# The last token tile's right half of the down projection as two pieces of 256 columns

## The chip, the core and the metric

The kernel is one program on one core of one Trainium2 chip. The metric is the device time of one execution in microseconds (us), taken as the median of several executions. The profile is of one more execution; its span runs from the first instruction to the last.

## The reference

The reference is one layer of a hybrid decoder on 512 tokens of 1024 channels: a norm, three parallel token mixers, gates, an output projection, and then a gated MLP with a short convolution. The change touches only the last two lines, the MLP's down projection with its residual and the final norm over each token's 1024 channels:

```python
def rms_norm(x, gain):
    x32 = x.astype(jnp.float32)
    y = x32 * lax.rsqrt(jnp.mean(x32 * x32, axis=-1, keepdims=True) + EPS)
    return (y * gain.astype(jnp.float32)).astype(x.dtype)
...
    x = x + (jax.nn.gelu(gate_h, approximate=True) * val_h) @ w_down[l]
return rms_norm(x, final_norm)
```

## The kernel before

The 512 tokens are four tiles of 128, t = 0 to 3; a tile is 128 partitions. The 1024 channels are two halves of 512 columns, c = 0 (left) and c = 1 (right). `x2[t][c]` holds the residual stream. Most of the down projection is added to `x2` earlier, by `down_fast`. What is left are the last 512 of its 3072 inner rows, `group(20)`, and this is the very end of the program: `down_units(wdown2, group(20), final, None, final_left, 2)`.

Each fp32 product is made of three matmuls by `mm3` (L104): both operands are split into a high and a low part, in the page's names `whi`/`wlo` or `r`. For a token tile and a half there are 2 weight tiles (`nk` = 2) of 2 blocks, so 4 terms and 12 matmuls of 128x512, all into one bank of PSUM, the accumulator memory.

The left halves are made first by `token_units`, for all four tiles in four banks. The right halves follow in `token_held`, tile by tile, each in a bank of its own. After each tile's 12 matmuls `evac` runs: DVE adds the bank into `x2[t][1]` (L1107), ACT squares it and sums along the row into `msq[t][:, 1:2]` (`meansq`, L124; the row READ_ACCUMULATOR belongs to it), and `final(t)` makes the row's scale `y`: a square root on ACT (L1378) and four small steps on DVE (L1379 to L1382, with `y` from L1382). The left half's part of the mean square came before, in `final_left(t)`, which also multiplied the left half by the gain on POOL (`xl`). Then the left half is scaled by `y` on ACT (L1389) and stored (L1390), and the right half is scaled on DVE by `y` and the gain (L1386, inner function `right`) and stored (L1387).

The order on DVE is set by hand around these steps. For t < 3, `final` puts its last DVE step (L1382) in `queue` and `right` in `late`. The next tile's `evac` takes them out: its add is issued after that step of the tile before, and the tile before's `right` is issued after the add. So DVE does, in this order: scale of tile t (L1379 to L1382), add of tile t + 1, `right` of tile t. For t = 3 `right` runs at once, and the left store goes out from ACT's queue; all other stores go out from SyncE's (SP's). Engines take their instructions in order, and a wait holds everything behind it on that engine.

Of the kernel before, what the change touches and what calls it, by code (L numbers as in the profile page):

```python
# [13 lines left out]
AF = mybir.ActivationFunctionType  # L14
ALU = mybir.AluOpType
# [3 lines left out]
P = 128  # L19
D = 1024  # L20
KD = D // P
S = 512
NT = S // P
# [34 lines left out]
def trunk(ctx: ExitStack, tc: tile.TileContext, x, xT, mem, memT, par, wdecay, wch, wv, wg, wmk,  # L58
          wmv, wrg, wbr, wout, wup, wdown, wdown2, gffn, gfin, out):
    nc = tc.nc  # L60
# [11 lines left out]
    def nm(s):  # L72
        uid[0] += 1
        return f"{s}_{uid[0]}"

    def fslot(shape=(P, S)):
        return apool.tile(list(shape), F32, tag="s", name=nm("f"))
# [7 lines left out]
    def bank(shape=(P, S)):  # L85
        return psm.tile(list(shape), F32, tag="mm", name=nm("mm"))

    def sbank(shape=(P, S)):
        return pss.tile(list(shape), F32, tag="sm", name=nm("sm"))

    def stat(n, p=P):
        return small.tile([p, n], F32, tag=f"st{n}", name=nm("st"), bufs=12)
# [7 lines left out]
    def mm3(ps, terms, first=True, last=True, more=False):  # L100

        seq = [p for a, b, c, d in terms for p in ((a, c), (a, d))] + [(b, c) for a, b, c, d in terms]
        for i, (l, r) in enumerate(seq):
            nc.tensor.matmul(ps, lhsT=l, rhs=r, start=first and i == 0,  # L104
                             stop=last and i == len(seq) - 1, skip_group_check=more)
# [15 lines left out]
    def meansq(src, acc, width):  # L121

        junk = small.tile([P, src.shape[-1]], BF16, tag="junk", name=nm("junk"), bufs=2)
        nc.scalar.activation(junk, src, AF.Square, scale=width ** -0.5, accum_out=acc)  # L124
# [8 lines left out]
    def unit(dram, n, fn, parts=1):  # L133

        w = {}
        i = sum(1 for k, *_ in prog if k == "unit")

        def ready():
            w["w"] = fetch(dram, n, parts)
            for h in behind.get(i, ()):  # L140
                h()
        prog.append(("unit", [(AHEAD, ready)], lambda: fn(w["w"])))
# [5 lines left out]
    def step(fn):  # L148
        prog.append(("step", [], fn))

    def weave(units, steps, lead=0):

        done, m = 0, max(1, len(units) - lead)
        for i, u in enumerate(units):
            unit(*u)
            upto = len(steps) * max(0, i + 1 - lead) // m
            for s in steps[done:upto]:
                step(s)
            done = max(done, upto)
        for s in steps[done:]:  # L160
            step(s)
# [36 lines left out]
    HB = D // 2  # L198
# [10 lines left out]
    ps = sbank((P, P))  # L209
# [38 lines left out]
    def token_units(dram, n, lhs, nt, evac, nk=4):  # L248

        pst = []  # L250

        def fn(i, w):
            if i == 0:
                pst.extend(bank((P, n)) for _ in range(nt))
            for t in range(nt):
                mm3(pst[t], [(*lhs(2 * i + j, t), *w(j, 2)) for j in range(2)], i == 0, i == nk - 1)
                if i == nk - 1:
                    evac(t, pst[t])
        return [(dram[i], 2 * n, lambda w, i=i: fn(i, w)) for i in range(nk)]

    def token_held(dram, n, lhs, nt, evac, between=None, nk=4):

        ws = []

        def fn(i, w):
            ws.append(w)
            if i < nk - 1:
                return
            for t in range(nt):
                ps = bank((P, n))  # L270
                for c in range(nk):
                    mm3(ps, [(*lhs(2 * c + j, t), *ws[c](j, 2)) for j in range(2)], c == 0, c == nk - 1)
                    if c == 0 and t >= 2 and between is not None:
                        between(t - 2)
                evac(t, ps)
        return [(dram[i], 2 * n, lambda w, i=i: fn(i, w), 2) for i in range(nk)]
# [274 lines left out]
    xr = [None] * NB  # L551
# [533 lines left out]
    x2 = [[None, None] for _ in range(NT)]  # L1085
# [6 lines left out]
    gb = {}  # L1092

    def gain_rows(src):
        for j in range(2):
            gb[j] = fslot()
            with tc.issue_after(loads[-1].ins):
                nc.sync.dma_start(gb[j], src[:, j * HB:(j + 1) * HB])

    msq, queue, late = {}, [], []  # L1100

    def down_units(wd, acts, after, between=None, left=None, nk=4):

        def evac(t, ps, c):

            with tc.issue_after(queue.pop()) if queue else ExitStack():
                add = nc.vector.tensor_tensor(out=x2[t][c], in0=x2[t][c], in1=ps, op=ALU.add)  # L1107
            while late:
                with tc.issue_after(add.ins):
                    late.pop()()  # L1110
            if c == 0:
                msq[t] = stat(2)
            meansq(x2[t][c], msq[t][:, c:c + 1], D)
            if c == 1:
                after(t)
            elif left is not None:
                left(t)
        lhs = lambda k, t: tuple(a[:, t * P:(t + 1) * P] for a in acts(k))
        add = lambda c: lambda t, ps: evac(t, ps, c)
        return token_units(wd[0], HB, lhs, NT, add(0), nk) + token_held(wd[1], HB, lhs, NT, add(1), between, nk)  # L1120

    def rstd(t):
        tot, ss = stat(1), msq.pop(t)
# [32 lines left out]

    step(lambda: gain_rows(gffn))
    wo = down_units(wout, lambda k: mr[k], norm2, norm2_flip)
    step(lambda: residual(0))
    weave(wo[:4], [])  # L1160
# [209 lines left out]

    lefts = {}

    def final(t):
        b, xl = lefts.pop(t)
        ss = msq.pop(t)

        root, h, y, u = stat(1), stat(1), stat(1), stat(1)
        nc.scalar.activation(root, ss[:, 1:2], AF.Sqrt, bias=b)  # L1378
        nc.vector.tensor_scalar(out=h, in0=ss[:, 1:2], scalar1=b, scalar2=-0.5, op0=ALU.add, op1=ALU.mult)  # L1379
        nc.vector.reciprocal(y, root)  # L1380
        nc.vector.scalar_tensor_tensor(out=u, in0=y, scalar=h, in1=y, op0=ALU.mult, op1=ALU.mult)
        last = nc.vector.scalar_tensor_tensor(out=y, in0=u, scalar=1.5, in1=y, op0=ALU.add, op1=ALU.mult)  # L1382

        def right():
            xr = fslot()
            nc.vector.scalar_tensor_tensor(out=xr, in0=x2[t][1], scalar=y, in1=gb[1], op0=ALU.mult, op1=ALU.mult)  # L1386
            nc.sync.dma_start(out[t * P:(t + 1) * P, HB:], xr)  # L1387

        nc.scalar.activation(xl, xl, AF.Copy, scale=y)  # L1389
        (nc.sync if t < NT - 1 else nc.scalar).dma_start(out[t * P:(t + 1) * P, :HB], xl)  # L1390
        if t < NT - 1:
            queue.append(last.ins)
            late.append(right)
        else:
            right()

    acts = {}

# [7 lines left out]
    group = lambda first: lambda k: acts[first + k]  # L1406
# [14 lines left out]
    blend(us[2:], down_fast(0, 3, group(0), True, False))  # L1421
    blend(up_units(range(20, NF), halves), down_fast(3, 2, group(12), False, True))
    step(lambda: gain_rows(gfin))
    weave(down_units(wdown2, group(20), final, None, final_left, 2), [])

    emit()

# [90 lines left out]
```

## Time and profile before

| | us |
|---|---|
| median of 3 runs | 923.41 |
| lowest and highest of them | 923.1, 926.32 |
| profiled execution, its own time | 924.37 |
| span of the profiled execution | 922.6 |
| end of the last matmul, from the start of the span | 915.66 |

The profiled execution's time is 1.8 us more than its span, and 0.96 us over the median. Rows give a start in us from the start of the span, then a length. Matmuls are pipelined: the next starts before the one before has ended, so the step from start to start is shorter than the length of one.

### The profile page before, as it was taken

To read this page: it belongs to the slowest core of one execution; us is meant where nothing else is said; L and a number is where in the kernel's file an instruction comes from. 1 tells how busy PE (TensorE), PEld (TensorE's weight loads), DVE (VectorE), ACT (ScalarE), POOL (GpSimd) and SP (SyncE) were. 2 spreads that over 40 slices of the span, in tenths; PEclk is the share of its full clock that TensorE was granted. 3 is DMA by queue.
4 is the path that set the end of the run, shared out by engine and by line. 5 is a ranking of instruction groups with operands and counts; after the bars stand their busy time and mean duration, and the time that the engine had idled before them with its cause. 6 is when DMAs were issued, how large, how long until landed. Compare 5 with 4: busy or idle time off the path is not lost.

```text
span 922.6 us, 12732 instructions
## 1 busy us (share of the span) xinstructions
PE 912.0 (99%) x4606; PEld 784.1 (85%) x4606; DVE 657.2 (71%) x1168; ACT 524.1 (57%) x888; POOL 128.1 (14%) x168
## 2 busy tenths in 40 slices
PE   9999999999999999999999999999999999999997
PEld 7899888888889998888888898998988888888885
DVE  6997755665689568746766678767787757598765
ACT  7765655685865468474534446555555445445544
POOL 0010000000243430320000000222111130013102
PEclk9999999999999999999999999999999999999998
DMA  7446223213467884321157313675646785357622
GB/s 238 148 137 214 92 88 101 88 42 119 110 170 167 187 204 126 115 86 53 52 157 258 116 59 90 157 185 130 148 114 165 145 228 125 114 137 181 139 69 91
DMA packets 51183, 123.27 MB, mean 134 GB/s; under 512 B 6145, under 2 KB 14001, under 8 KB 51121
## 3 DMA queue, kind: packets, MB, share of 16 engines
q1 hardware_dynamic: 35648, 94.99, 31.6%
q0 software_dynamic: 15328, 27.21, 17.3%
q8 instruction: 36, 0.59, 0.3%
q10 hardware_dynamic: 144, 0.26, 0.1%
q14 instruction: 27, 0.21, 0.1%
HBM read 117.99 MB, written 3.67 MB: 132 GB/s over the span
## 4 chain that ended last, share of the span: by engine, by line
PE 87%; DMA 5%; DVE 3%; issue 2%; ACT 2%; POOL 0%; SPq 0%; DVEq 0%; POOLq 0%; ACTq 0%
PE mm L104 78%; DMA f<-in_wup 4%; PE sm L104 3%; DMA f<-in_wv 2%; PE mm L436 2%; DVE wlo L98 1%; DVE r L98 1%; ACT r L97 1%; PE sm L211 0%; PE sm L996 0%; PE sm L983 0%; PE sm L1010 0%; DVE f L810 0%; PE sm L1147 0%; PE sm L601 0%
## 5 line engine op out<-in xcount | busy, mean ns | idle before, releaser
L97 ACT ACTIVATE whi<-raw 128x1024 fp32r<-128x1024 f32 (+3 forms) x142 | 135.5, 961 | 144.4 <-PE mm L104 113.1
L98 DVE TENSOR_TENSOR wlo<-raw,whi 128x1024 fp32r<-128x1024 f32 (+3 forms) x142 | 157.4, 1113 | 82.8 <-ACT whi L97 39.4
L104 PE MATMUL mm<-whi,r 128*128 128x512 f32 (+2 forms) x568 | 171.2, 372 | 0.0
L104 PEld LDWEIGHTS mm<-whi,r 128*128 128x128 f32 x568 | 105.5, 188 | 15.9 <-ACT r L97 0.3
L104 PE MATMUL mm<-hh,whi 128*128 128x512 f32 x288 | 113.4, 394 | 0.0
L104 PE MATMUL mm<-hl,whi 128*128 128x512 f32 x288 | 112.8, 392 | 0.0
L104 PE MATMUL mm<-wlo,r 128*128 128x512 f32 (+2 forms) x284 | 105.7, 372 | 0.5 <-DVE wlo L98 0.5
L104 PE MATMUL mm<-h2l,whi 128*128 128x512 f32 x264 | 102.8, 390 | 0.0
L104 PE MATMUL mm<-h2h,whi 128*128 128x512 f32 x264 | 102.7, 390 | 0.0
L98 DVE TENSOR_TENSOR r<-f,r 128x512 fp32r<-128x512 f32 (+3 forms) x144 | 79.7, 577 | 23.0 <-ACT r L97 22.7
L104 PE MATMUL mm<-r,whi 128*128 128x512 f32 (+1 forms) x432 | 94.2, 367 | 0.0
L97 ACT ACTIVATE r<-f 128x512 fp32r<-128x512 f32 (+3 forms) x144 | 70.1, 535 | 34.1 <-DMA f<-in_wup 29.2
L98 DVE TENSOR_TENSOR wlo<-f,whi 128x512 fp32r<-128x512 f32 (+2 forms) x90 | 53.8, 631 | 47.5 <-ACT whi L97 40.6
L104 PEld LDWEIGHTS mm<-r,whi 128*128 128x128 f32 x432 | 75.2, 189 | 13.1
L97 ACT ACTIVATE whi<-f 128x512 fp32r<-128x512 f32 (+2 forms) x90 | 48.2, 579 | 62.5 <-PE mm L104 48.8
L104 PE MATMUL mm<-hh,wlo 128*128 128x512 f32 x288 | 71.4, 390 | 0.0
L104 PE MATMUL mm<-r,r 128*128 128x512 f32 (+2 forms) x336 | 65.7, 346 | 0.3 <-ACT r L97 0.3
L104 PE MATMUL mm<-h2h,wlo 128*128 128x512 f32 x264 | 65.2, 389 | 0.0
L104 PEld LDWEIGHTS mm<-hh,wlo 128*128 128x128 f32 x288 | 54.0, 188 | 11.2
L104 PEld LDWEIGHTS mm<-hh,whi 128*128 128x128 f32 x288 | 54.1, 188 | 10.8
L104 PEld LDWEIGHTS mm<-hl,whi 128*128 128x128 f32 x288 | 54.1, 188 | 10.7
L104 PEld LDWEIGHTS mm<-r,r 128*128 128x128 f32 (+1 forms) x336 | 53.3, 186 | 9.6 <-ACT r L97 0.5
(261 smaller groups left out, 1545.2 us busy)
## 6 DMA issues: line engine op xcount, KB each, us to landing
raw<-in_wch SPq DMA_DIRECT2D x39, 512.0 KB, 3.3
raw<-in_wup SPq DMA_DIRECT2D x36, 512.0 KB, 4.0
f<-in_wdown POOLq DMA_DIRECT2D x40, 256.0 KB, 7.0
raw<-in_wbr SPq DMA_DIRECT2D x24, 384.0 KB, 3.1
raw<-in_wdown SPq DMA_DIRECT2D x14, 512.0 KB, 3.8
f<-in_wup SPq DMA_DIRECT2D x24, 256.0 KB, 6.9
f<-in_wup POOLq DMA_DIRECT2D x24, 256.0 KB, 6.4
f<-in_wdown SPq DMA_DIRECT2D x20, 256.0 KB, 4.7
```

What stands on the lines that cost most here:

```text
L97: nc.scalar.activation(hi, src, AF.Copy)
L98: return (eng or nc.vector).tensor_tensor(out=lo, in0=src, in1=hi.bitcast(F32), op=ALU.subtract)
L104: nc.tensor.matmul(ps, lhsT=l, rhs=r, start=first and i == 0, stop=last and i == len(seq) - 1, skip_group_check=more)
L436: nc.tensor.matmul(ps[u], lhsT=w(a, u, k), rhs=xs["r"][k][j], start=k == 0 and i < n, stop=k == KD - 1 and i >= len(seq) - n)
```

## The change

Tile 3's right half is made in two pieces of 256 columns, h = 0 and 1, in the two halves of the same bank: 12 matmuls of 128x256 for the first piece, then 12 for the second. After each piece `last` adds the 256 columns into `x2[3][1]` and squares them. The first piece's square sum goes to `msq[3]` as before; `final_quarter` adds it to the left half's on DVE and gives the second piece a sum of its own. The second piece then calls `final(3)`, which makes `y` as before, and scales both halves in pieces of 256 columns, each with a store of its own (128 KB in place of 256 KB): one store from ACT's queue, three from SP's. `queue` and `late` are emptied at the first piece's add.

```diff
+                if last is not None and t == nt - 1:
+                    for h in range(2):
+                        cols = slice(h * n // 2, (h + 1) * n // 2)
+                        mm3(ps[:, cols], [(*lhs(2 * c + j, t), *(a[:, cols] for a in ws[c](j, 2)))
+                                          for c in range(nk) for j in range(2)])
+                        last(cols, ps[:, cols])
+                    return
...
+        def last(cols, ps):
+            t, x = NT - 1, x2[NT - 1][1][:, cols]
+            with tc.issue_after(queue.pop()) if queue else ExitStack():
+                add = nc.vector.tensor_tensor(out=x, in0=x, in1=ps, op=ALU.add)
+            while late:
+                with tc.issue_after(add.ins):
+                    late.pop()()
+            meansq(x, msq[t][:, 1:2], D)
+            (quarter if cols.start == 0 else after)(t)
...
+    def final_quarter(t):
+        b, xl = lefts[t]
+        lefts[t] = stat(1), xl
+        nc.vector.tensor_tensor(out=lefts[t][0], in0=b, in1=msq[t][:, 1:2], op=ALU.add)
+        msq[t] = stat(2)
...
+        xr = fslot()
+        for h in range(2):
+            c = slice(h * HB // 2, (h + 1) * HB // 2)
+            nc.scalar.activation(xl[:, c], xl[:, c], AF.Copy, scale=y)
+            nc.vector.scalar_tensor_tensor(out=xr[:, c], in0=x2[t][1][:, c], scalar=y, in1=gb[1][:, c],
+                                           op0=ALU.mult, op1=ALU.mult)
+            (nc.scalar if h else nc.sync).dma_start(out[rows, c], xl[:, c])
+            nc.sync.dma_start(out[rows, HB + c.start:HB + c.stop], xr[:, c])
...
-    weave(down_units(wdown2, group(20), final, None, final_left, 2), [])
+    weave(down_units(wdown2, group(20), final, None, final_left, 2, final_quarter), [])
```

On every engine the order up to tile 3's right half is the same. The line numbers of the changed kernel are higher: its add of a piece is L1130, the sum of the squares L1395, the scale L1404 to L1407, `right` of tile 2 L1413 and of tile 3 L1427. In brackets stands the engine whose count an instruction waits for.

On PE, before, tile 3's right half (bank `mm_8649`) begins so:

```order
L104 MATMUL mm_8649<-r_8458,r_7878 128x512 [waits DVE_49]
L104 MATMUL mm_8649<-r_8459,r_7878 128x512
L104 MATMUL mm_8649<-r_8462,r_8072 128x512
L104 MATMUL mm_8649<-r_8463,r_8072 128x512
L104 MATMUL mm_8649<-r_8458,r_7879 128x512
```

On PE, in the changed kernel, the last three matmuls of the first piece and the first three of the second:

```order
L104 MATMUL mm_8649<-r_8462,r_8073 128x256
L104 MATMUL mm_8649<-r_8496,r_8229 128x256
L104 MATMUL mm_8649<-r_8500,r_8411 128x256
L104 MATMUL mm_8649<-r_8458,r_7878 128x256 [waits DVE_49]
L104 MATMUL mm_8649<-r_8459,r_7878 128x256
L104 MATMUL mm_8649<-r_8462,r_8072 128x256
```

There are now 24 matmuls of half the columns, and the second piece's first one waits for DVE; in the built program the count that it waits for is that of the first piece's add.

On DVE, before, from the last step of tile 2's scale to the end of the program (`m_4828` is tile 3's right half, `f_8663` tile 2's result):

```order
L1382 SCALAR_TENSOR_TENSOR st_8640<-st_8641,st_8640 128x1 [waits DVE_49]
L1107 TENSOR_TENSOR m_4828<-m_4828,mm_8649 128x512 [waits PE_49]
L1386 SCALAR_TENSOR_TENSOR f_8663<-m_4826,st_8640,f_8454 128x512 [waits DVE_49]
L1379 TENSOR_SCALAR st_8669<-st_8555,st_8558 128x1 [waits Activation_49]
L1380 RECIPROCAL st_8670<-st_8668 128x1 [waits Activation_49]
L1381 SCALAR_TENSOR_TENSOR st_8671<-st_8670,st_8669 128x1 [waits DVE_49]
L1382 SCALAR_TENSOR_TENSOR st_8670<-st_8671,st_8670 128x1 [waits DVE_49]
L1386 SCALAR_TENSOR_TENSOR f_8679<-m_4828,st_8670,f_8454 128x512 [waits DVE_49]
```

On DVE, in the changed kernel, the same stretch:

```order
L1407 SCALAR_TENSOR_TENSOR st_8640<-st_8641,st_8640 128x1 [waits DVE_49]
L1130 TENSOR_TENSOR m_4828<-m_4828,mm_8649 128x256 [waits PE_49]
L1413 SCALAR_TENSOR_TENSOR f_8663<-m_4826,st_8640,f_8454 128x512 [waits DVE_49]
L1395 TENSOR_TENSOR st_8668<-st_8558,st_8555 128x1 [waits Activation_49]
L1130 TENSOR_TENSOR m_4828<-m_4828,mm_8649 128x256 [waits PE_49]
L1404 TENSOR_SCALAR st_8687<-st_8670,st_8668 128x1 [waits Activation_49]
L1405 RECIPROCAL st_8688<-st_8686 128x1 [waits Activation_49]
L1406 SCALAR_TENSOR_TENSOR st_8689<-st_8688,st_8687 128x1 [waits DVE_49]
L1407 SCALAR_TENSOR_TENSOR st_8688<-st_8689,st_8688 128x1 [waits DVE_49]
L1427 SCALAR_TENSOR_TENSOR f_8695<-m_4828,st_8688,f_8454 128x256 [waits DVE_49]
L1427 SCALAR_TENSOR_TENSOR f_8695<-m_4828,st_8688,f_8454 128x256
```

The first piece's add stands where the whole add stood, behind tile 2's scale; the second piece's add stands behind tile 2's `right` and behind L1395, which waits for ACT's square of the first piece.

On SP, in the changed kernel, the last six stores (`f_8633`, `f_8546` and `f_8663` are of tiles 1 and 2, `f_8695` is tile 3's right half, `f_8560` its left):

```order
L1414 DMA out<-f_8633 128x512 [waits DMAHW4_49,DVE_49]
L1418 DMA out<-f_8546 128x512 [waits DMAHW5_49,Activation_49]
L1414 DMA out<-f_8663 128x512 [waits DMAHW6_49,DVE_49]
L1430 DMA out<-f_8695 128x256 [waits DMAHW7_49,DVE_49]
L1429 DMA out<-f_8560 128x256 [waits DMAHW1_49,Activation_49]
L1430 DMA out<-f_8695 128x256 [waits DMAHW2_49,DVE_49]
```

Where one store of tile 3 stood there are three; the fourth, of the left half's second piece, is ACT's.

## Rows read from the trace of the kernel before

**Rows 1.** The page: busy share of PE, and the engines' shares of the chain.

```profile
PE 912.0 (99%) x4606; PEld 784.1 (85%) x4606; DVE 657.2 (71%) x1168; ACT 524.1 (57%) x888; POOL 128.1 (14%) x168
...
PE 87%; DMA 5%; DVE 3%; issue 2%; ACT 2%; POOL 0%; SPq 0%; DVEq 0%; POOLq 0%; ACTq 0%
```

**Rows 2.** The chain that ended last, from 912.8 us: start, length, what.

```profile
912.72 2.96 PE mm L104 x13
...
915.70 0.70 DVE m L1107
...
916.42 0.73 ACT junk L124 x2
...
918.21 0.72 ACT f L1389
```

**Rows 3.** Timeline of PE, the four right halves: start, length, operation, count.

```profile
904.62 11.04 PE L104 MATMUL mm<-r,r 128*128 128x512 f32 x48
```

**Rows 4.** Timeline of the end, ACT, DVE and the stores' issues.

```profile
915.24 0.16 DVE L1382 SCALAR_TENSOR_TENSOR st<-st,st 128x1 f32<-128x1 f32 x1
915.50 0.72 ACT L1389 ACTIVATE f<-f,st 128x512 f32<-128x512 f32 x1 [0.74 <-DVE st L1382]
915.70 0.69 DVE L1107 TENSOR_TENSOR m<-m,mm 128x512 f32<-128x512 f32 x1 [0.30 <-PE mm L104]
...
916.30 0.74 DVE L1386 SCALAR_TENSOR_TENSOR f<-m,st,f 128x512 f32<-128x512 f32 x1
916.42 0.63 ACT L124 ACTIVATE junk<-m 128x512 bf16<-128x512 f32 x1 [0.20 <-DVE m L1107]
...
918.15 0.75 DVE L1386 SCALAR_TENSOR_TENSOR f<-m,st,f 128x512 f32<-128x512 f32 x1
...
918.96 0.37 ACTq L1390 DMA_DIRECT2D out<-f  x1
```

**Rows 5.** Timeline of PE at 640 us: twelve matmuls of 256 columns in a row.

```profile
640.24 1.60 PE L104 MATMUL mm<-r,r 128*128 128x256 f32 x12
```

**Rows 6.** Timeline around 628 us: PE waits for DVE's read of a bank.

```profile
628.16 0.41 DVE L1278 TENSOR_TENSOR f<-f,mm 128x256 f32<-128x256 f32 x1
...
628.72 0.36 PE L104 MATMUL mm<-h2h,r 128*128 128x256 f32 x1 [0.68 <-DVE f L1278]
...
628.91 0.28 PE L104 MATMUL mm<-h2l,r 128*128 128x256 f32 x1
```

**Rows 7.** Groups with shapes apart: count | busy us, mean ns of one | idle before.

```profile
L1278 DVE TENSOR_TENSOR f<-f,mm 128x256 f32<-128x256 f32 x12 | 5.0, 414 | 0.2 <-PE mm L104 0.2
...
L464 DVE SCALAR_TENSOR_TENSOR r<-raw,prm,r 128x256 fp32r<-128x256 f32 x8 | 3.7, 480 | 0.0
...
L124 ACT ACTIVATE junk<-f 128x192 bf16<-128x192 f32 x16 | 5.6, 353 | 5.8 <-DVE f L1015 5.8
...
L463 ACT ACTIVATE r<-raw,prm 128x256 fp32r<-128x256 f32 x8 | 3.4, 497 | 0.0
```

**Rows 8.** Stretches at the end; the last two columns are DMA share and GB/s.

```profile
919.50:920.00 0.50, 0.00 (x0) 0.00 (x0) 0.00 (x0) 0.00 (x0) 0.00 (x0) 0.50 0.46 172
...
920.50:921.00 0.50, 0.00 (x0) 0.00 (x0) 0.00 (x0) 0.00 (x0) 0.00 (x0) 0.50 1.02 381
...
921.25:922.60 1.35, 0.00 (x0) 0.00 (x0) 0.00 (x0) 0.00 (x0) 0.00 (x0) 0.50 0.00 0
```

**Rows 9.** SP's timeline at the start, three issues in a row.

```profile
1.74 1.37 SPq L423 DMA_DIRECT2D raw<-in_wch  x3
```

**Rows 10.** DMA: GB/s in 40 slices; issues: count, KB each, us to landing.

```profile
GB/s 238 148 137 214 92 88 101 88 42 119 110 170 167 187 204 126 115 86 53 52 157 258 116 59 90 157 185 130 148 114 165 145 228 125 114 137 181 139 69 91
...
raw<-in_wch SPq DMA_DIRECT2D x12, 128.0 KB, 4.1
```

**Rows 11.** Stretches behind the last matmul; PEclk is the third column from the right.

```profile
917.50:918.00 0.50, 0.00 (x0) 0.00 (x0) 0.43 (x3) 0.00 (x0) 0.00 (x0) 0.83 0.69 246
918.00:918.50 0.50, 0.00 (x0) 0.00 (x0) 0.46 (x2) 0.29 (x1) 0.00 (x0) 0.50 1.03 389
```

More of the change, by code (lines that the diff above doesn't have):

```diff
@@ L259, in token_units, with token_held @@
         return [(dram[i], 2 * n, lambda w, i=i: fn(i, w)) for i in range(nk)]
-    def token_held(dram, n, lhs, nt, evac, between=None, nk=4):
+    def token_held(dram, n, lhs, nt, evac, between=None, nk=4, last=None):
         ws = []
@@ L1100, in trunk, with down_units @@
     msq, queue, late = {}, [], []
-    def down_units(wd, acts, after, between=None, left=None, nk=4):
+    def down_units(wd, acts, after, between=None, left=None, nk=4, quarter=None):
         def evac(t, ps, c):
@@ L1117, in evac @@
                 left(t)
+        def last(cols, ps):
[7 more added lines that the diff above has]
+            (quarter if cols.start == 0 else after)(t)
         lhs = lambda k, t: tuple(a[:, t * P:(t + 1) * P] for a in acts(k))
         add = lambda c: lambda t, ps: evac(t, ps, c)
-        return token_units(wd[0], HB, lhs, NT, add(0), nk) + token_held(wd[1], HB, lhs, NT, add(1), between, nk)
+        return token_units(wd[0], HB, lhs, NT, add(0), nk) + token_held(wd[1], HB, lhs, NT, add(1), between, nk,
+                                                                          None if quarter is None else last)
     def rstd(t):
@@ L1382, in final @@
         last = nc.vector.scalar_tensor_tensor(out=y, in0=u, scalar=1.5, in1=y, op0=ALU.add, op1=ALU.mult)
+        rows = slice(t * P, (t + 1) * P)
         def right():
@@ L1386, in right @@
             nc.vector.scalar_tensor_tensor(out=xr, in0=x2[t][1], scalar=y, in1=gb[1], op0=ALU.mult, op1=ALU.mult)
-            nc.sync.dma_start(out[t * P:(t + 1) * P, HB:], xr)
-        nc.scalar.activation(xl, xl, AF.Copy, scale=y)
-        (nc.sync if t < NT - 1 else nc.scalar).dma_start(out[t * P:(t + 1) * P, :HB], xl)
+            nc.sync.dma_start(out[rows, HB:], xr)
         if t < NT - 1:
+            nc.scalar.activation(xl, xl, AF.Copy, scale=y)
+            nc.sync.dma_start(out[rows, :HB], xl)
             queue.append(last.ins)
             late.append(right)
-        else:
-            right()
+            return
+        xr = fslot()
[6 more added lines that the diff above has]
+            nc.sync.dma_start(out[rows, HB + c.start:HB + c.stop], xr[:, c])
     acts = {}
```

## The prediction, made before the changed kernel ran

> **What bounds the kernel now.** I read the page first. PE is busy 99% of the span and 87% of the chain is PE [rows 1], so for nearly all of it the time is PE's, and the change leaves that part alone. The end is another matter. The chain from 912.8 us [rows 2] shows what ended last: PE up to 915.68, then one thing behind another: add on DVE, square on ACT, square root and small DVE steps, scale of the left half on ACT at 918.21. From 915.68 to the end of the span, 922.6, are 6.9 us in which PE has nothing to do. The reader should see there that this tail is a chain of single steps, so a step shortened in it counts in full, and so does any delay of the last matmul.
>
> The stretches at the end [rows 8] show the rest: the last stores begin to move in the half us from 919.5 (0.46 of it busy, so from some 919.75), run at up to 381 GB/s, and in the last 1.35 us no byte moves. The timeline [rows 4] shows what decides the case: DVE makes tile 2's scale until 915.40 (915.24 + 0.16), and only 0.30 us later, when PE is done, adds tile 3. So DVE has little room before the last tile's add.
>
> **PE, first piece.** 48 matmuls of 512 columns take 11.04 us [rows 3]. With 0.39 for the length of the last, the step is (11.04 - 0.39) / 47 = 0.227 us. Tile 3 begins after 36 of them, at 904.62 + 36 x 0.227 = 912.78. Twelve matmuls of 256 columns take 1.60 us with the same operands' shapes [rows 5], so a step of (1.60 - 0.28) / 11 = 0.120: half of the columns cost 53% of the time. The first piece ends at 912.78 + 11 x 0.120 + 0.28 = 914.38. The 24 steps cost 2.88 us where 12 cost 2.72; this alone is 0.16 us.
>
> **The first add and the wait.** The add of the first piece stands on DVE behind tile 2's scale, which ends at 915.40 [rows 4], and nothing of tile 2's chain is moved by the change. So PE's early end at 914.38 buys nothing here: the add runs from 915.44 to 915.85, at 0.41 us for 128x256 out of PSUM (the first of [rows 7]). And the order shows that the second piece's first matmul waits for it, since both pieces lie in one bank. The trace has the same step once [rows 6]: DVE reads a bank until 628.57, PE goes on at 628.72, 0.15 us later, and its second matmul follows after 0.19 in place of 0.12. So the second piece runs from 916.00 to 916.00 + 0.07 + 11 x 0.120 + 0.28 = 917.67, and PE is idle for 1.6 us before it. That is the main term: the last matmul ends **2.0 us later** than the 915.66 of before. Behind PE's wait nothing is queued but this piece; who waits for it is DVE's last add.
>
> What hides the rest: the first piece's square on ACT (behind the 0.72 us of tile 2's left half from 915.50, so from 916.24), tile 2's `right` on DVE (0.74 us, now from 915.85, its store 0.45 us earlier) and L1395 are all done by some 917.0, beside the second piece's matmuls. They cost nothing as long as the second piece ends after 917.0.
>
> **What the tail gains.** The second add takes 0.41 in place of 0.69, from 917.71 to 918.12. The square of 512 columns takes 0.63 [rows 4], of 192 columns 0.353 [rows 7]; 256 lie at 0.41, so 0.22 less. The square ends at 918.65, against 917.15 [rows 2]: of 2.0 us 0.5 are won back, **1.5 remain**. The root and the four small steps are as before: 1.00 us up to the scale of the right half, so 919.65 in place of 918.15 [rows 4].
>
> **Scale and stores.** A first piece on DVE takes 0.48 in place of 0.75, on ACT 0.50 in place of 0.72 [rows 4, 7]. So the first store, of the right half's first piece, can be issued on SP at 920.16, where both of before went out at some 918.95 (the scales end at 918.90 and 918.93, and ACT issues at 918.96 [rows 2, 4]). SP has three issues in a row; three take 1.37 us at the start of the program with 0.43 for the last [rows 9], a step of 0.47. They go out at 920.16, 920.63 and 921.10, while ACT sends the fourth at some 920.7. Before, bytes moved 0.8 us after the issue, from 919.75 [rows 8], and 512 KB at 381 GB/s take 1.38 us, to some 921.15. Now they move from 920.95; at the same rate 512 KB would end at 922.33, and the third store of SP, 128 KB from 921.90, at 922.24: both say **922.3**. Then 1.35 us as before [rows 8]: the span ends at about 923.65, **1.1 us later** than the 922.55 to 922.6 of before. So of the 1.5 us the pieces win 0.4 back, because the first bytes move sooner after `y`; the issues in a row cost most of what could be won.
>
> **Sum.** +2.0 (last matmul) - 0.28 (add) - 0.22 (square) - 0.4 (scale and stores) = +1.1 us. The profiled execution's 924.37 would become 925.5; it stands 0.96 above the median, so for the median 923.41 + 1.1 = **924.5**. Bounds: if the handover is 0.05 and the issues step by 0.40, +0.8; if SP's last waits for the stores come one behind another, or ACT's pieces are slower than the row, +1.6. So 924.2 to 925.0 for this case.
>
> The Trainium skill has a rule that speaks against this change: "PSUM — Partial Sum Buffer", section Terms, says that TensorE writing and VectorE reading one bank in the same partitions at once is an error, wherever in the bank they are. By that rule the pieces can't run beside each other in one bank, and it would be the 924.5 above; if columns counted, it would be the 923.8 of the first rival. The trace agrees as far as it goes: the one place where DVE reads a bank that PE goes on writing has PE waiting 0.68 us [rows 6].
>
> **Rivals.** (1) The pieces overlap as the change's words say: PE does not wait, the second piece ends at 912.78 + 23 x 0.120 + 0.28 = 915.82. Even then DVE's order holds the second add: first add until 915.85, `right` of tile 2 until 916.6, L1395 behind the first square (ACT is free at 916.24, so 916.75), second add 917.0 to 917.4, square until 917.9, 0.75 later than before; less the 0.4 of the stores, +0.4: **923.8**. For it: the columns are apart. Against it: the wait in the order.
>
> (2) Slower: the clock. PE now idles 1.6 us, from 914.38 to 916.0. In the span no wait of PE behind its first microseconds is longer than the 0.68 us of [rows 6]. The only fall of the clock came behind the last matmul: it ended at 915.66, and the granted clock is a mean of 0.83 in the half us from 917.5 and 0.50 in the next [rows 11], so it fell at about 917.83, 2.2 us later. 1.6 is under 2.2, which speaks against it; that PE's first idle of this length comes here speaks for it. If the second piece runs at 1.2 GHz and not 2.4, its 12 steps cost 12 x 0.12 = 1.44 us more: **925.9**. It decides if the granted clock is at 0.5 anywhere from 916.0 to 917.7.
>
> (3) Slower: the stores. A row of a piece is 1 KB, of before 2 KB. No store of the trace has rows of 1 KB; the nearest is the first slice of the span at 238 GB/s, with the 12 loads of 128 KB, which have such rows, among others [rows 10]. At that rate 512 KB take 2.2 us and not 1.38: +0.8, **925.3**.
>
> Gone faster than 923.4 needs something that I do not see: with no wait at all the DVE's order still costs 0.4.
>
> **How the numbers follow.** Forecast 0.65, first rival 0.10, clock 0.12, stores 0.08, other 0.05. The range takes the first three in and some of the spread of the runs of before (923.1 to 926.32): 923.3 to 926.2. A measurement of this kernel can tell about 0.5%, 4.6 us, from no change. All cases lie within it, so same 0.97, slower 0.02, faster 0.01.
>
> **What would show it.** Right, if in the changed profile PE's second group of twelve starts some 0.15 us after the first add's end, with an idle of about 1.6 us before it that DVE ended; if the last matmul ends near 917.7 in place of 915.66; if the second square ends near 918.65; if three stores on SP start about 0.47 us apart, and the span ends near 923.65. Wrong, if the two groups stand without a gap (first rival), if the second takes 2.9 us (clock), if bytes move at 240 GB/s at the end (stores), or if tile 2's scale on DVE is moved, on whose 915.40 the first add rests.

## The result

| | before | changed |
|---|---|---|
| median of 22 runs each, us | 925.54 | 927.0 |
| lowest to highest | 922.14 to 927.31 | 924.63 to 930.27 |
| ratio | | 1.0022, 95% interval 1.0014 to 1.003 |
| profiled execution, span | 922.6 | 922.8 |

The changed kernel is slower by about 2.0 us (the ratio's 0.22% of 925.5, interval 1.3 to 2.8; the two medians alone lie 1.46 us apart). That is inside the 0.5% which the prediction called no change, but more than its +1.1, and the absolute time lies over its range of 923.3 to 926.2. Two things went wrong, and they are separate: a term of the sum, and the number on which the sum was put. The median of before was 923.41 with the first three runs, 925.54 with 22, 924.83 and 926.07 in the two later sets.

The two profiled spans differ by only 0.2 us, since what lies ahead of the change varies from execution to execution. So I count every length from one instruction that both kernels have and that nothing of the change reaches: the end of tile 2's scale on DVE, called A below. A is 915.40 in before ([rows 4], 915.24 + 0.16) and 913.58 in the changed kernel. From A to the end of the span it is 7.15 us in before and 9.23 in the changed kernel: +2.08, which lies within the interval of the measured difference.

### The profile page after: what moved, and what is told of

Its sections match the earlier page's. It is cut to its first block, busy times and chain, and to the rows that moved or that the text cites. A ratio compares the mean times of both kernels' runs of the same rounds, so it can differ in the third digit from the quotient of the medians.

```text
span 922.8 us, 12767 instructions
## 1 busy us (share of the span) xinstructions
PE 911.2 (99%) x4618; PEld 784.3 (85%) x4618; DVE 657.8 (71%) x1171; ACT 525.2 (57%) x891; POOL 128.0 (14%) x168
## 4 chain that ended last, share of the span: by engine, by line
PE 93%; DVE 3%; ACT 2%; issue 1%; DMA 1%; SPq 0%; ACTq 0%
PE mm L104 84%; PE sm L104 4%; PE mm L444 2%; DVE wlo L98 1%; ACT r L97 0%; DMA f<-in_wup 0%; DVE f L400 0%; PE sm L1004 0%; PE sm L991 0%; DMA raw<-in_wch 0%; PE sm L1018 0%; PE sm L609 0%; DVE r L98 0%; PE sm L1166 0%; DVE hl L98 0%
## 5 line engine op out<-in xcount | busy, mean ns | idle before, releaser
L104 PE MATMUL mm<-r,r 128*128 128x256 f32 (+2 forms) x348 | 66.0, 340 | 1.6 <-DVE m L1130 1.4
```

## The profile after

The timeline of the changed kernel's end. The rows of before are in [rows 4].

```profile
913.42 0.16 DVE L1407 SCALAR_TENSOR_TENSOR st<-st,st 128x1 f32<-128x1 f32 x1
913.50 0.41 DVE L1130 TENSOR_TENSOR m<-m,mm 128x256 f32<-128x256 f32 x1
913.67 0.72 ACT L1417 ACTIVATE f<-f,st 128x512 f32<-128x512 f32 x1 [0.74 <-DVE st L1407]
913.83 0.74 DVE L1413 SCALAR_TENSOR_TENSOR f<-m,st,f 128x512 f32<-128x512 f32 x1
913.96 1.69 PE L104 MATMUL mm<-r,r 128*128 128x256 f32 x12 [1.41 <-DVE m L1130]
914.30 0.40 ACT L124 ACTIVATE junk<-m 128x256 bf16<-128x256 f32 x1
...
915.69 0.42 DVE L1130 TENSOR_TENSOR m<-m,mm 128x256 f32<-128x256 f32 x1 [0.70 <-PE mm L104]
916.15 0.42 ACT L124 ACTIVATE junk<-m 128x256 bf16<-128x256 f32 x1 [1.35 <-DVE m L1130]
...
917.66 0.88 DVE L1427 SCALAR_TENSOR_TENSOR f<-m,st,f 128x256 f32<-128x256 f32 x2
917.72 0.91 ACT L1426 ACTIVATE f<-f,st 128x256 f32<-128x256 f32 x2 [0.74 <-DVE st L1407]
918.18 0.33 SPq L1430 DMA_DIRECT2D out<-f  x1
918.60 0.39 SPq L1429 DMA_DIRECT2D out<-f  x1
918.66 0.37 ACTq L1429 DMA_DIRECT2D out<-f  x1
919.08 0.40 SPq L1430 DMA_DIRECT2D out<-f  x1
```

Read from the top: the first add starts when tile 2's scale is nearly through, though PE has been done with the first piece for a microsecond (since 913.96 - 1.41 = 912.55); the second twelve matmuls sit behind a hole of 1.41 us that DVE's add (L1130) ended; the last add starts 2.11 us behind A, where before it started 0.30 behind it. In before PE's last matmul was at A + 0.26, here it ends at A + 2.07.

The chain of the changed kernel, from 912.6 us, has turned round: it no longer comes down PE into the tail, but through tile 2's chain on ACT and DVE, then the first add, then PE. In [rows 2] PE had the stretch up to 915.68 to itself.

```profile
912.64 0.30 ACT st L1403
...
913.42 0.16 DVE st L1407
913.58 0.34 DVE m L1130
913.92 0.04 issue
913.96 1.70 PE mm L104 x12
...
915.69 0.43 DVE m L1130
```

Stretches of the changed kernel at the end; the last two columns are DMA share (the mean busy share of the DMA engines) and GB/s, as in [rows 8].

```profile
919.00:919.50 0.50, 0.00 (x0) 0.00 (x0) 0.00 (x0) 0.00 (x0) 0.00 (x0) 0.50 0.82 262
919.50:920.00 0.50, 0.00 (x0) 0.00 (x0) 0.00 (x0) 0.00 (x0) 0.00 (x0) 0.50 0.97 328
920.00:920.50 0.50, 0.00 (x0) 0.00 (x0) 0.00 (x0) 0.00 (x0) 0.00 (x0) 0.50 1.02 338
920.50:920.75 0.25, 0.00 (x0) 0.00 (x0) 0.00 (x0) 0.00 (x0) 0.00 (x0) 0.50 0.71 242
920.75:922.81 2.06, 0.00 (x0) 0.00 (x0) 0.00 (x0) 0.00 (x0) 0.00 (x0) 0.50 0.02 4
```

With the DMA engines as busy as before (share 1.02) the stores now move 338 GB/s where they moved 381. And behind 920.75, where the last store has no more to move, 2.06 us pass to the end of the span, where it was 1.35 (the 4 GB/s of that row are one packet of 8 KB at 922.56, on the queue of kind `instruction`, not of a store). Part of that is an instruction of SP itself. The instructions DRAIN of the program's last line, on SP, first of before, then of the changed kernel (least, median and most ns of one):

```profile
L1514 SPq DRAIN  x3: 7/7/7, 921.7 to 922.0; - x3
```

```profile
L1549 SPq DRAIN  x3: 7/7/130, 921.6 to 922.3; - x3
```

One of three drains takes 130 ns in place of 7, and the trace has it begin 0.34 us behind the one before, in place of 0.05.

## The experiments

All of them in one table first: us from A, by each kernel's one trace. "Landing" is the moment when the last store of tile 3 is counted as done on its semaphore, the counter that a finished transfer raises.

| | last matmul ends | tile 3's scale ends | last landing | span ends |
|---|---|---|---|---|
| before | 0.26 | 2.71 | 6.22 | 7.15 |
| changed | 2.07 | 4.05 | 7.57 | 9.23 |
| mm_only | 0.41 | 2.86 | 6.36 | 7.29 |
| compute_only | 2.08 | 4.05 | 7.56 | 8.49 |
| stores_only | 0.26 | 2.71 | 6.22 | 7.89 |
| two_banks | 0.42 | 2.83 | 6.35 | 8.02 |
| more_stores_early | 0.26 | 2.72 | 6.26 | 7.68 |
| sp_shorter | 2.08 | 4.05 | 7.58 | 8.79 |

Columns that an edit should not touch agree to some 0.04 us from kernel to kernel, so one trace of each is enough for differences of tenths. (reordered, the last run, moves A itself and is counted from another instruction.) The time is a much blunter tool: A itself lies anywhere from 913.6 to 918.5 in these traces, and an interval is some 1.5 to 3 us wide.

**Each piece in a bank of its own (two_banks).** It takes away what PE waits for.

```diff
-                ps = bank((P, n))
+                ps = bank((P, n)) if last is None or t < nt - 1 else None
...
+                        ps = sbank((P, n))
```

(`sbank` takes a bank from the kernel's other set of banks, once for each piece.)

> The changed kernel with each piece of tile 3's right half in a bank of its own, nothing else. All lengths are counted from the end of tile 2's scale on DVE (before: 915.40, changed: 913.58), since the stretch ahead of it varies from run to run. Theory (the wait for the bank is the main term): the second twelve matmuls follow the first without a gap, the last matmul ends 0.4 us behind tile 2's scale in place of 2.07 (before 0.26); tile 3's scale ends at about 2.85 in place of 4.05 (before 2.71), held now by ACT, which scales tile 2's left half first; the span ends at about 8.0 in place of 9.23 (before 7.15). Rival (the wait costs nothing at the end, the stores set it): the span still ends at about 9.2. Time against the kernel before: theory +0.9 us, rival +2.0.

Measured: the span ends at 8.02; ratio to before 1.0009 (0.9992 to 1.0026), so +0.8 us with -0.7 to +2.4. The 24 matmuls stand in a row, and the second add follows the first by a microsecond:

```profile
913.85 3.03 PE L104 MATMUL sm<-r,r 128*128 128x256 f32 x24
...
916.38 0.41 DVE L1131 TENSOR_TENSOR m<-m,sm 128x256 f32<-128x256 f32 x1
...
916.72 0.75 DVE L1414 SCALAR_TENSOR_TENSOR f<-m,st,f 128x512 f32<-128x512 f32 x1
...
917.38 0.41 DVE L1131 TENSOR_TENSOR m<-m,sm 128x256 f32<-128x256 f32 x1
917.50 0.19 ACT L124 ACTIVATION_READ_ACCUMULATOR junk<-m 128x1 f32 x1
```

The wait is worth 1.21 us at the end (9.23 to 8.02), so it was a term that counts in full. But the last matmul comes 1.65 us sooner, so 0.44 of it is caught further on: the second add starts at A + 0.91, though PE was done at 0.42, since `right` of tile 2 stands ahead of it on DVE. (The expectation named ACT as what holds tile 3. ACT does square the first piece only behind tile 2's left half, but it is through at 917.69, 0.1 us before the second add ends at 917.79, so DVE is what holds it.) So even without the wait the two pieces don't get tile 3's scale done any sooner than before (2.83 against 2.71): the pieces' adds and squares lie on engines that tile 2 still holds. Whether the built program waits because both pieces lie in one bank or because they are parts of one buffer, this run doesn't tell apart: it changes both.

**Only scale and stores in pieces (stores_only).** The kernel before with the second half of `final` as the change writes it.

```diff
+        for h in range(2):
+            c = slice(h * HB // 2, (h + 1) * HB // 2)
+            nc.scalar.activation(xl[:, c], xl[:, c], AF.Copy, scale=y)
+            nc.vector.scalar_tensor_tensor(out=xr[:, c], ...)
+            (nc.scalar if h else nc.sync).dma_start(out[rows, c], xl[:, c])
+            nc.sync.dma_start(out[rows, HB + c.start:HB + c.stop], xr[:, c])
```

> The kernel before with only tile 3's scale and stores in pieces of 256 columns; its matmuls, add and square are whole. Theory: tile 3's scale ends 2.71 us behind tile 2's, as before, and from there to the end of the span it is as in the changed kernel, 5.18 us in place of 4.44: the span ends at 7.9 behind tile 2's scale (before 7.15), +0.75 us. Rival (my prediction's step: stores in pieces win 0.4 us): it ends at about 6.75, -0.4 us. Second rival (the longer end of the changed kernel is chance of that one profile): as the first rival.

Measured: 7.89, ratio 0.9997 (0.9981 to 1.0014). The trace is where the theory put it. The interval reaches from -1.8 to +1.3 us, so the times can't tell +0.74 from nothing. This is the step of my prediction that fell: by the trace, pieces win nothing. Tile 3's scale ends at the same place and the last store lands at the same place, 6.22, to the hundredth; then come 0.74 us more. Why the landing stays: the first store is issued 0.27 us sooner than before, but SP's three issues start 0.42 and 0.48 us apart, so the last goes out 0.6 us later than before, and the bytes move slower (no run takes these two apart):

```profile
922.90:923.40 0.50, 0.00 (x0) 0.00 (x0) 0.00 (x0) 0.00 (x0) 0.00 (x0) 0.50 1.02 340
923.40:923.90 0.50, 0.00 (x0) 0.00 (x0) 0.00 (x0) 0.00 (x0) 0.00 (x0) 0.50 0.99 334
```

**All but that (compute_only).** The changed kernel with scale and stores whole again, its `final` being that of before.

```diff
-        for h in range(2):
-            c = slice(h * HB // 2, (h + 1) * HB // 2)
-            ...
+        nc.scalar.activation(xl, xl, AF.Copy, scale=y)
+        (nc.sync if t < NT - 1 else nc.scalar).dma_start(out[t * P:(t + 1) * P, :HB], xl)
```

> The changed kernel with tile 3's scale and stores whole, as before; matmuls, adds and squares stay in pieces in one bank. Theory: tile 3's scale ends at 4.05 us behind tile 2's as in the changed kernel, and from there 4.44 us to the end as before: 8.5 in all, +1.35 us over before, and 0.75 us less than the changed kernel. Rival (stores in pieces win 0.4 us, so that taking them away costs that): 9.6 in all.

Measured: 8.49, ratio 1.0011 (0.9996 to 1.0026), by which the times can't tell +1.34 from nothing either. In the traces the two halves of the change add up: +1.34 here and +0.74 in stores_only make +2.08. Its gap on PE is the same as in the changed kernel:

```profile
917.63 1.69 PE L104 MATMUL mm<-r,r 128*128 128x256 f32 x12 [1.41 <-DVE m L1130]
```

**The narrow matmuls alone (mm_only).** Both pieces in one bank with no add between them, then the whole add.

```diff
+                for h in range(2 if nk == 2 and t == nt - 1 else 0):
+                    cols = slice(h * n // 2, (h + 1) * n // 2)
+                    mm3(ps[:, cols], [(*lhs(2 * c + j, t), *(a[:, cols] for a in ws[c](j, 2)))
+                                      for c in range(nk) for j in range(2)])
```

> The kernel before with tile 3's right half made by 24 matmuls of 256 columns in one bank, both pieces done before the one whole add; add, square, scale and stores as before. It prices the narrower matmuls alone. Theory (0.12 us a step): the last matmul ends 0.41 us behind tile 2's scale in place of 0.26, and the span ends at 7.30 in place of 7.15. Rival (narrow matmuls cost more, or a second piece started in a bank that holds the first costs time by itself): the last matmul ends at 0.6 or later.

Measured: last matmul at 0.41, the span ends at 7.29 (A is 916.16 + 0.16 here):

```profile
915.73 1.00 PE L104 MATMUL mm<-r,r 128*128 128x256 f32 x7
...
916.16 0.16 DVE L1386 SCALAR_TENSOR_TENSOR st<-st,st 128x1 f32<-128x1 f32 x1
...
916.77 0.69 DVE L1111 TENSOR_TENSOR m<-m,mm 128x512 f32<-128x512 f32 x1 [0.45 <-PE mm L104]
```

Twenty-four matmuls of 256 columns cost 0.15 us more than twelve of 512, as [rows 5] said they would (0.16), and a second group begun in the bank of a finished first one costs nothing of itself. What costs is the wait for the read between them.

**More stores on SP, but early (more_stores_early).** Where do the 0.74 us behind the last landing come from?

```diff
+        if t < 2:
+            for c in (slice(0, HB // 2), slice(HB // 2, HB)):
+                nc.sync.dma_start(out[t * P:(t + 1) * P, c], xl[:, c])
+        else:
             (nc.sync if t < NT - 1 else nc.scalar).dma_start(out[t * P:(t + 1) * P, :HB], xl)
```

> The kernel before with the left stores of tiles 0 and 1 in two pieces of 256 columns each; tile 3 is as before. This gives SP the two more stores of the changed kernel, but early, where nothing waits for them, so only what comes behind the last store can differ: which of SP's last waits the last stores answer, and how SP's end goes. Theory (the longer end of the changed kernel comes from the last store being waited for in the middle of SP's row of waits, with five still to come at 0.06 us each): from the last store's landing to the end of the span 1.25 us in place of 0.93 (changed kernel 1.67). Rival (it comes from two more instructions on SP's queue at its end): 1.67. Second rival (from the stores' own shape): 0.93.

Measured: from the last landing to the end 1.42 us, between theory and rival, and both turn out to be at work. Tile 3's stores are whole here, so their shape is not the cause. The trace shows SP, at the end of the program, waiting for its eight DMA semaphores in a fixed order, one each 0.06 us. The stores take these semaphores in turn. In before the last landing is on the last of the eight, so the other seven waits are over by then. Two stores more move it, early ones too: here it is on the second, and six waits are still to come behind it (0.44 us from the landing to the end of the last wait, where it was 0.07). Of the 0.49 us over before's 0.93 that is 0.37. The rest, 0.12, is the late instruction:

```profile
L1518 SPq DRAIN  x3: 7/7/137, 921.1 to 921.7; - x3
```

It is the third drain here and the second in the changed kernel. Here it costs only 0.12, since most of its lateness falls into a wait that SP has there anyway (its last instruction starts 0.15 us behind that drain, in before 0.45). Counted through SP's instructions in the trace, it is in both the 464th, and so in stores_only and two_banks. Before, compute_only, mm_only and reordered have 462 instructions on SP and end before it.

**Fewer instructions on SP (sp_shorter).** If the place costs it, the changed kernel must lose it with a shorter SP.

```diff
-                nc.sync.dma_start(gb[j], src[:, j * HB:(j + 1) * HB])
+                nc.scalar.dma_start(gb[j], src[:, j * HB:(j + 1) * HB])
```

> The changed kernel with the loads of both gain rows, long before the end, issued by ACT in place of SP: four loads, so that SP's instructions are six fewer in all, 461 in place of 467; the stores and SP's last waits are the same. In the four kernels with more than 463 instructions on SP, that of place 463 begins 0.34 us late and takes 0.13; before and compute_only have 462 and show none. Theory (the place in SP's instructions costs it): no such instruction here, and from the last store's landing to the end of the span 1.3 us in place of 1.67, the span ending at 8.85 behind tile 2's scale in place of 9.23. Rival (it comes from the stores in pieces): 1.67 and 9.23 again.

Measured: 461 instructions on SP, from the last landing to the end 1.21 us, the span ends at 8.79. The slow drain is gone, with the same stores and the same waits:

```profile
L1549 SPq DRAIN  x3: 7/7/7, 926.5 to 926.8; - x3
```

So of the 0.73 us by which the changed kernel's end behind the last landing is longer than before (1.66 against 0.93), 0.45 belong to the place of an instruction among SP's own, and 0.28 to the order of the waits (five of them behind the landing). The traces have the same step once more, 128 instructions earlier: SP's 336th instruction begins 0.34 us behind the end of the one before in all nine traces, at 644.86 in before, 642.07 in the changed kernel and 645.61 in sp_shorter, where another instruction stands at that place. What the chip does at these places stays open. This kernel's time, 929.1 in one run, is that of an execution whose A lies at 918.5.

**What the change meant to do (reordered).** Two banks, tile 3's scale and stores whole, and tile 2 out of the way: the first add is no longer put behind tile 2's scale, and tile 2's left half is scaled behind tile 3's square root.

```diff
-            with tc.issue_after(queue.pop()) if queue else ExitStack():
+            with tc.issue_after(queue.pop()) if queue and cols.start else ExitStack():
                 add = nc.vector.tensor_tensor(out=x, in0=x, in1=ps, op=ALU.add)
...
+        while left_late:
+            with tc.issue_after(sq.ins):
+                left_late.pop()()
```

> What the change set out to do, with its three obstacles taken away: two banks; the first piece's add no longer held behind tile 2's scale; tile 2's left half scaled on ACT behind tile 3's square root, and its right half on DVE behind the second add; scale and stores of tile 3 whole. Counted from the start of tile 2's add (before: end of the span at 9.57, changed kernel 11.65). Theory: second add ends at 3.30, square at 3.83, tile 3's scale at 4.8 in place of 5.13, the span ends at 9.25, 0.3 us less than before. Rival (the small steps on ACT and DVE get in each other's way and give it back): 9.55 or more. Neither can be told from no change by the time; the trace decides.

Measured: 9.27 from the start of tile 2's add, against 9.57 in before. Ratio to before 0.9987 (0.9972 to 1.0002). The trace has the 0.3 us. The times lean the same way, and their interval just includes no change, so a gain is shown by the trace alone.

```profile
916.80 0.42 DVE L1131 TENSOR_TENSOR m<-m,sm 128x256 f32<-128x256 f32 x1
...
917.14 0.21 DVE L1408 TENSOR_SCALAR st<-st,st 128x1 f32<-128x1 f32 x1
...
918.24 0.42 DVE L1131 TENSOR_TENSOR m<-m,sm 128x256 f32<-128x256 f32 x1 [0.28 <-PE sm L104]
918.58 0.74 DVE L1415 SCALAR_TENSOR_TENSOR f<-m,st,f 128x512 f32<-128x512 f32 x1
918.69 0.42 ACT L124 ACTIVATE junk<-m 128x256 bf16<-128x256 f32 x1 [0.93 <-DVE m L1131]
```

Now the first add (916.80) comes ahead of tile 2's small steps, which it holds up by less than 0.1 us (A lies 2.50 us behind the start of tile 2's add, in before 2.42), and the second add waits for PE again and for nothing else.

## Why the prediction was right and wrong

**PE's price: right.** 0.16 us for the narrower matmuls, 0.15 measured in mm_only.

**The hold and the wait: right in kind, a little too large.** The first add did start at tile 2's scale (A - 0.08, not A + 0.04), took 0.41, and PE went on 0.05 us behind it, not 0.15; so 1.41 us of idle and not 1.6, and the last matmul 1.8 later than before and not 2.0. The handover of [rows 6] was the wrong row to take: there PE waits for two engines, DVE and ACT, and in the trace an instruction that only waits (628.61 to 628.66) stands between the add and the weight load; here there is none. That two_banks takes the wait away confirms its cause. Of the rule of the Trainium skill that I weighed ("PSUM — Partial Sum Buffer", section Terms) no run here can show more than this: with one bank PE waited, with two it did not, and the forecast hung on the built program's wait, not on the rule. [rows 6] could not speak for it either: there DVE reads the same columns of the bank that PE goes on writing.

**Add and square: right.** 0.28 and 0.22 were forecast; tile 3's scale ended 1.34 us later than before, 0.47 less than the last matmul.

**Scale and stores: wrong, and this is the failed term.** The step said -0.4 us; stores_only says +0.74. Two parts of it failed. First, I let the pieces move at the rate of the whole stores, 381 GB/s, and put the slower rate in a rival, at 238 and +0.8 by a slice that had other work in it. The true rate lies between, 334 to 340, and together with SP's issues in a row it just eats the early start: the landing did not move at all. That part of the term should have been 0. Second, I carried the 1.35 us behind the last byte over "as before". It became 2.06. I had named SP's waits one behind another as a bound, but priced the whole bound at +0.5 together with ACT; the waits alone are 0.28 by the difference of sp_shorter and before, and the late instruction, 0.45, was not in my account at all. In the trace of before SP ends two instructions ahead of that place; what it does have is the same step at SP's 336th instruction. So +0.4 and +0.74 make the 1.1 us by which the term missed; the computing part was 0.16 too high, and 1.1 became 2.08.

**The range: wrong for another reason.** The sum was put on a median of three runs, 923.41, and the range was drawn to hold 923.3 to 926.2. The three runs themselves reached from 923.1 to 926.32, and I took the middle of them for known to a few tenths. (The 4.6 us that the prediction gave as the least to be told from no change were too much: 22 runs of each kernel told 2.0.) Had the sum been put on 925.54, the 927.6 of the measured shift and my own 926.6 would both lie near the 927.0. The spread arises ahead of the change: by the same instruction, A, the traces differ by 5 us. Counted by single instructions of DVE that all the kernels have, 1.6 of the 1.8 us between before and the changed kernel, and 3.4 of the 4.6 between stores_only and the changed kernel, arise between 560 and 700 us. (Of compute_only's 3.7 us 2.0 arise in the first 40.) In the stretch from 600 to 700 us PE's busy time in three traces (before, changed, stores_only; second number, of 100 us) is not the same:

```profile
600.00:700.00 100.00, 99.28 (x608) 89.00 (x608) 77.37 (x135) 55.83 (x100) 19.35 (x22) 1.00 0.64 147
```

```profile
600.00:700.00 100.00, 100.00 (x614) 89.97 (x613) 78.22 (x136) 56.88 (x101) 19.04 (x22) 1.00 0.65 148
```

```profile
600.00:700.00 100.00, 98.40 (x605) 87.53 (x604) 75.78 (x132) 55.12 (x99) 20.18 (x23) 1.00 0.62 141
```

What makes PE wait there in one execution and not in the next stays open.

**The rivals.** (1) The overlap: the wait was there, so it did not come. Its price of +0.4 was off as well: with the wait gone two_banks ends 0.87 later than before, 0.12 from the computing and the rest from the stores; the second add came sooner than I had it, since L1395 no longer stood ahead of it. (2) The clock: it did not fall. In the changed kernel the second twelve matmuls ran at the full level, 2.4 GHz, behind 1.41 us without a matmul (PEclk, third column from the right):

```profile
912.60:913.90 1.30, 0.00 (x0) 0.00 (x0) 1.08 (x6) 0.53 (x3) 0.00 (x0) 1.00 0.89 331
913.90:915.70 1.80, 1.69 (x12) 1.49 (x12) 0.84 (x4) 0.90 (x3) 0.00 (x0) 1.00 0.36 134
```

(3) The stores' rate: true in part, as told. That the change makes less than 0.5% was right, and so was the sign.

## What to carry to other kernels

Work moved beside other work is worth what the engine it goes to has free at that moment: here the early piece of PE's result met a DVE and an ACT that the tile before still held, and a bank whose second piece had to wait for the read of the first. Cutting the last store into pieces starts it sooner, but adds issues in a row, narrower rows and waits at the end; ask what happens behind the last byte as well. And before a time is forecast to a microsecond, look at how far the runs shown lie apart; a change in a tail of 7 us is better measured in the trace, from an instruction that it does not touch, than by the clock on the wall.

## What the runs showed of the hardware

- With the DMA engines fully busy (share 0.99 to 1.02), stores of 128 KB with rows of 1 KB moved 334 to 340 GB/s (changed kernel, stores_only); stores of 256 KB with rows of 2 KB 381 (before).
- The 464th instruction of SP in the trace began 0.34 to 0.36 us behind the end of the one before (in before such a drain begins 0.05 to 0.08 behind it) and took 0.13 to 0.14 us where its like take 0.007, in all four kernels that were longer than that (changed, two_banks, stores_only, more_stores_early), and in none that was shorter. In all nine traces the 336th, too, began 0.34 us behind the end of the one before.
- PE went on 0.05 us after the end of the DVE add that it had waited for (changed kernel; 913.91 to 913.96).
- PE's granted clock stayed at its full level, 2.4 GHz, over 1.41 us without a matmul (changed kernel).
